# A pair of experts in which the transposes of the hidden rows move between two gathers and two down chunks change banks

## The chip, the cores and the metric

The kernel runs on one core of one Trainium2 chip. The metric is the device time of one execution in microseconds; of the kernel before, the median of three runs is 1393.09 us (1392.07 to 1394.43). TensorE (PE in the profile) multiplies matrices and writes to banks of PSUM; VectorE (DVE) and ScalarE (ACT) read the banks and write to SBUF; GpSimd (POOL) works on SBUF; SyncE (SP) issues the transfers from HBM.

## The reference, cut to what matters

The reference is one layer of a hybrid model on 256 tokens of width 2048: attention with compressed, selected and windowed keys beside a state-space mixer, an output projection with a norm, then a mixture of 32 experts and a second norm. The change lies in the experts. Each token is routed to two of the 32, and each expert is a gated unit of width 512:

```python
def expert_block(args):
    tok, e = args
    xb = h[tok]
    return (jax.nn.silu(xb @ w_gate[e]) * (xb @ w_up[e])) @ w_down[e]
...
out = jnp.zeros((n, d), jnp.float32).at[buf_tok].add(y.reshape(buf_len, d) * buf_w[:, None])
```

All of it is float32, and all 32 experts' weights are read: 3 x 2048 x 512 x 4 bytes each, 402.7 MB together.

## The kernel before, in words

The part ahead of the experts (projections, attention, state-space, output projection, first norm, routing) takes the first 425 us and is left as it is.

The experts are worked on in 16 pairs. Each expert has 64 slots for its tokens, so the two of a pair share the 128 columns or partitions of a tile. Tokens are picked by one-hot matrices: `one_hots(pr)` (line 1114 on) builds S, and `gather(xg, S, c)` (line 1120 on) multiplies the normed rows `hpm` by S into one bank, 16 records on TensorE for each quarter c of the model's width, and evicts the result with the norm's gain and offset into `xg`; VectorE evicts quarters 0 and 2, ScalarE quarters 1 and 3. A pair then runs, in the order in which the loop of line 1292 issues the work:

- the gate products `p_gate` and the up products `p_up` (line 1300), four chunks each of two weight tiles. An fp32 matmul shows as two records in the trace, so a chunk is 16 records and the eight chunks 128;
- `hidden` (line 1185 on), a generator in two steps. The first step is silu of the gate on ScalarE and the product with up on VectorE. The second transposes the result by four matmuls against the identity into the bank `p_ht` and copies it to `aT` on ScalarE;
- the first two quarters of the next pair's gather, between the generator's two steps;
- `weights_t` (line 1133 on): the one-hot matrices transposed and the slots' weights, by TensorE into the bank `p_sw`, and three copies on ScalarE to `swT` and `wsl`;
- four down chunks `p_dn` (line 1330), each with a matmul group into a bank, then `weighted` (lines 1152 and 1153: ScalarE scales by the slots' weights and rounds, VectorE keeps the rest) and, one chunk later, `combine` (lines 1161 and 1165: TensorE multiplies by `swT`, VectorE adds to the sums of the tokens). The next pair's quarters 2 and 3 are gathered behind the first and ahead of the last `combine`.

Each engine works through its instructions in the order of the program, so this order of issue is also each engine's queue. PSUM's eight banks are given out by tags, in turn within a tag: three "acc" (down chunks, combines), two "s" (gate, up), two "t" (gathers), one "o" (`p_ht`, `p_sw`). A matmul into a bank waits until its last reader is done.

The weights go through a ring of SBUF tiles of 1 MB (line 944 on). `ring_fill` issues on SP the next tiles as soon as a matmul chunk has used up others, so a transfer starts when a tile is free, up to a lane of semaphores: SP holds eight of these, and waits for the transfer that used the lane before. A pair has 24 tiles of 1024 KB. In the last pair the tiles are half as large, and the down chunks are eight of 256 columns. `besides` (line 1282) names work that is issued behind a chunk of the gate or up products, `weights_t` of the last pair among it.

Of the kernel before, what the change touches and what calls it, by code (L numbers as in the profile page):

```python
# [32 lines left out]
NE = 32  # L33
# [37 lines left out]
def block_kernel(ctx: ExitStack, tc: tile.TileContext, I: dict, out: bass.AP):  # L71
# [10 lines left out]
    def bank(tag, name, dt=F32):  # L82
        return ps.tile([P, 512], dt, name=name, tag=tag, bufs=BANKS[tag])
# [3 lines left out]
    def slot(i, name, dt=F32):  # L87
        if i > 20:
            return extra[0].tile([P, 2048], dt, name=name, tag=f"s{i}")
        return big.tile([P, 2048], dt, name=name, tag=f"s{i}")  # L90
# [263 lines left out]
    acc = {}  # L354
# [575 lines left out]
    LASTP = NE // 2 - 1  # L930
# [44 lines left out]
    def ring_take(*key):  # L975
        t, at = ring["tiles"].pop(key)
        shared = any(o == at for _, o in ring["tiles"].values())
        if at not in ACC and at != WORK and not shared:
            ring["free"].append(at)
        return t  # L980

    def ring_fill():
        while ring["next"] < len(items) and (ring["free"] or second(ring["next"])):
            ring_load()
# [71 lines left out]
    def residual(j, a):  # L1056

        c = j % 4
        v = acc[a][:, 512 * c:512 * c + 512]
        if j < 4:  # L1060
            t = v if c in FIRST else bank("acc", "p_rt")
            dve.tensor_tensor(t.rearrange("p (q k) -> p q k", k=KT), hv[a][:, 32 * c:32 * c + 32],
                              RES[j].rearrange("p (q k) -> p q k", k=KT), op=OP.mult)
            if c not in FIRST:
                dve.tensor_add(v, v, t)
        else:
            dve.tensor_tensor(v, v, RES[j], op=OP.add)
# [46 lines left out]
    def one_hots(pr):  # L1114
        S = mw.tile([P, 2, P], F32, name="S", bufs=2)
        dve.tensor_tensor(S.rearrange("p a (u s) -> p a u s", u=2), slots[:, None, None, :CAP].to_broadcast([P, 2, 2, CAP]),
                          R[:, :, 2 * pr:2 * pr + 2, None].to_broadcast([P, 2, 2, CAP]), op=OP.is_equal)
        SEL[pr] = S

    def gather(dst, S, c, tags=("t",)):  # L1120
        pgs = [bank(t, "p_g") for t in tags]
        at = lambda k: pgs[k * len(tags) // 4][:, k * P:(k + 1) * P]
        for k in range(4):
            for a in range(2):
                pe.matmul(at(k), hpm[a][:, 4 * c + k], S[:, a], start=(a == 0), stop=(a == 1))  # L1125
        for k in range(4):
            kk = 4 * c + k
            if c % 2:
                act.activation(dst[:, kk], at(k), AF.Identity, scale=ln1[:, 0, kk:kk + 1], bias=ln1[:, 1, kk:kk + 1])
            else:  # L1130
                dve.tensor_scalar(dst[:, kk], at(k), ln1[:, 0, kk:kk + 1], ln1[:, 1, kk:kk + 1], op0=OP.mult, op1=OP.add)

    def weights_t(pr):
        S = SEL.pop(pr)
        pt = bank("o", "p_sw")
        for a in range(2):
            pe.transpose(pt[:, a * P:(a + 1) * P], S[:, a], ident)
        for a in range(2):
            pe.matmul(pt[:, T:T + 2], S[:, a], wt[:, a, 2 * pr:2 * pr + 2], start=(a == 0), stop=(a == 1),
                      skip_group_check=True)  # L1140
        swT = mw.tile([P, T], F32R, name="swT")
        wsl = mw.tile([P, 1], F32, name="wsl")
        act.copy(swT, pt[:, :T])
        for u in range(2):
            act.copy(wsl[64 * u:64 * u + 64], pt[64 * u:64 * u + 64, T + u:T + u + 1])
        SW[pr] = swT, wsl

    def weighted(py, wsl, i):

        w = py.shape[-1]  # L1150
        hi, lo = [WK[0][:, 512 * j:512 * j + w] for j in (i % 2, 2 + i % 2)]
        act.activation(hi, py, AF.Copy, scale=wsl)  # L1152
        dve.scalar_tensor_tensor(lo, py, wsl, f(hi), op0=OP.mult, op1=OP.subtract)  # L1153
        return hi, lo

    def combine(swT, ys, lo, w, fin=None, init=False):
        s = slice(lo, lo + w)
        for a in range(2):
            pc = bank("acc", "p_co")[:, :w]
            for y, part in enumerate(ys):  # L1160
                pe.matmul(pc, swT[:, a * P:(a + 1) * P], part, start=(y == 0), stop=(y == 1))  # L1161
            if init:
                dve.tensor_copy(acc[a][:, s], pc)
            else:
                dve.tensor_add(acc[a][:, s], acc[a][:, s], pc)  # L1165
            if fin:
                for h in range(lo, lo + w, 256):
                    dve.bn_stats(st2[:, a, h // 256], acc[a][:, h:h + 256])
# [16 lines left out]
    def hidden(pg, pu, xg):  # L1185

        am, aT = xg[:, 8:12].rearrange("p k s -> p (k s)"), xg[:, 12:16]
        act.activation(am, pg, AF.Silu)  # L1188
        dve.tensor_mul(am, am, pu)  # L1189
        yield  # L1190
        pt = bank("o", "p_ht")
        for q in range(4):
            pe.transpose(pt[:, q * P:(q + 1) * P], am[:, q::4], ident)
        act.copy(aT, pt.rearrange("p (q s) -> p q s", q=4))
        yield aT
# [73 lines left out]
    def rows2(j):  # L1269
        if j % 4 == 0:  # L1270
# [10 lines left out]
    ring_fill()  # L1281
    besides = {(0, "g", 0): [(gather, xg, SEL[0], 1), (gather, xg, SEL[0], 2)], (0, "g", 1): [(gather, xg, SEL[0], 3)],
               (0, "u", 0): [(weights,)],
               (1, "u", 0): [(block_table,)], (LASTP, "u", 0): [(weights_t, LASTP)],
               (LASTP - 1, "g", 0): [(split_rows2,)]}
    for j in range(2, 8):
        besides[j, "g", 0] = [(res_rows, j)]
        besides[j, "g", 1] = [(residual, j, 0)]
# [3 lines left out]
    for pr in range(NE // 2):  # L1292
        pg, pu = bank("s", "p_gate"), bank("s", "p_up")
        for nm, pp in (("g", pg), ("u", pu)):
            for q in GU[pr == LASTP]:
                tl = [ring_take(nm, 2 * pr + u, q) for u in range(2)]
                for k in range(q[1]):
                    kk = q[0] + k
                    for u in range(2):
                        pe.matmul(pp[64 * u:64 * u + 64, :], xg[:, kk, 64 * u:64 * u + 64], tl[u][:, k],  # L1300
                                  start=(kk == 0), stop=(kk == KT - 1), skip_group_check=True)
                ring_fill()
                for fn, *args in besides.get((pr, nm, (q[0] + q[1]) / 4 - 1), []):
                    fn(*args)
        if pr < LASTP:
            one_hots(pr + 1)
        if pr == 0:
            WK[0] = slot(WORK, "work", F32R)
        xg = slot(XGS, "xg").rearrange("p (k s) -> p k s", s=P)
        hid = hidden(pg, pu, xg)  # L1310
        next(hid)
        if pr < LASTP:
            gather(xg, SEL[pr + 1], 0)
            gather(xg, SEL[pr + 1], 1)
        if pr == 0:
            for a in range(2):
                acc[a] = slot(ACC[a], f"sum{a}")
            for j in FIRST:
                for a in range(2):
                    residual(j, a)  # L1320
        aT = next(hid)
        if pr < LASTP:
            weights_t(pr)
        late = None
        for i, (c, lo, w) in enumerate(DOWN_LAST if pr == LASTP else DOWN):
            tl = [ring_take("d", 2 * pr + u, (lo, w)) for u in range(2)]
            py = bank("t" if pr == LASTP else "acc", "p_dn")[:, :w]
            for q in range(4):
                for u in range(2):
                    pe.matmul(py[64 * u:64 * u + 64, :], aT[:, q, 64 * u:64 * u + 64], tl[u][:, q], start=(q == 0),  # L1330
                              stop=(q == 3), skip_group_check=True)
            ring_fill()
            ys = weighted(py, SW[pr][1], i)
            if late:
                combine(*late)
            if pr < LASTP and c in (0, 3):
                gather(xg, SEL[pr + 1], 2 + (c == 3))
            late = (SW[pr][0], ys, lo, w, pr == LASTP, pr == 0 and c not in FIRST)
        if pr < LASTP:
            combine(*late)  # L1340
        else:
            combine_last(sums_first(*late[2:4]), *late[:4])
        SW.pop(pr)
# [5 lines left out]
    with tc.For_i(0, nblk, 1) as b:  # L1349
# [29 lines left out]
        for src, pp in ((wgate, pg), (wup, pu)):  # L1379
            for q in range(4):  # L1380
                t = slot(OVER[n % 4], "w_o")
                n += 1
                nc.sync.dma_start(t, src[bass.ds(e, 1), q].rearrange("o p x -> p (o x)"))
                t = t.rearrange("p (k f) -> p k f", f=FE)
# [3 lines left out]
        hid = hidden(pg, pu, slot(XGS, "oam").rearrange("p (k s) -> p k s", s=P))  # L1388
        next(hid)
        aT = next(hid)  # L1390
        for c in range(4):
            t = slot(OVER[n % 4], "w_o")
            n += 1
            nc.sync.dma_start(t, wdown[bass.ds(e, 1), c].rearrange("o p x -> p (o x)"))
            t = t.rearrange("p (f d) -> p f d", f=4)
            py = bank("acc", "p_dn")
# [96 lines left out]
```

## Time and profile before

| | |
|---|---|
| median of three runs | 1393.09 us |
| the profiled execution, its own time | 1393.33 us |
| its span | 1391.6 us |
| TensorE busy | 1312.2 us, 94% |
| VectorE, ScalarE, GpSimd busy | 513.8, 357.2, 154.1 us |
| gate, up and down products, busy | 225.9, 222.9, 241.4 us |
| gathers, busy | 127.2 us |
| read from HBM | 468.79 MB |
| weight tiles, of gate, up and down each | 120 of 1024 KB and 16 of 512 KB |

The span runs from the first to the last instruction; 1.73 us of the execution lie around it. A busy share is a mean over the whole program, whose stages have different limits: what a change in one of them is worth has to be read from that stage's own windows, waits and transfers. "Landing" is the time at which a transfer's semaphore tells that its bytes are there.

### The profile page before, as it was taken

The numbers are of one execution on the slowest core, as the hardware profiler recorded it, in microseconds if no ns is written. First come the engines' busy times: TensorE is split into PE (matmuls) and PEld (weight loads), VectorE is DVE, ScalarE is ACT, GpSimd is POOL, SyncE is SP. The second block draws the span as 40 slices with busy tenths as digits, with TensorE's granted clock in tenths as the row PEclk, the third lists the DMA queues.
The fourth block names the chain that finished last, engine by engine and source line by source line (L and its number), as shares of the span: only waits on it lengthen the run. The fifth ranks groups of instructions, "written<-read, shape, count | busy, mean of one in ns | idle before, by whom it ended". The sixth has DMA issues, their size and how long they took to land. (4 is left out here: it accounts for less than half of the span.)

```text
span 1391.6 us, 18135 instructions
## 1 busy us (share of the span) xinstructions
PE 1312.2 (94%) x7347; PEld 758.6 (55%) x7347; DVE 513.8 (37%) x1085; ACT 357.2 (26%) x687; POOL 154.1 (11%) x78
## 2 busy tenths in 40 slices
PE   7998999999999999999999999999999999999994
PEld 6778899997885434344344443444434444344432
DVE  6757676468833323131121312213122131221207
ACT  5554566455424102011010111101111011110112
POOL 2533233333520000000000000000000000000001
PEclk9999999999999999999999999999999999999997
DMA  8752334435798899999999999999999999999981
GB/s 314 288 177 91 122 103 141 152 122 212 302 412 342 350 391 421 421 421 421 421 421 421 421 421 421 421 421 421 421 421 421 421 421 421 421 420 421 407 325 61
DMA packets 70692, 472.10 MB, mean 339 GB/s; under 512 B 8510, under 2 KB 8766, under 8 KB 17102
## 3 DMA queue, kind: packets, MB, share of 16 engines
q1 hardware_dynamic: 70016, 470.75, 83.6%
q8 instruction: 59, 0.97, 0.3%
q10 hardware_dynamic: 590, 0.17, 0.1%
q14 instruction: 27, 0.22, 0.0%
HBM read 468.79 MB, written 2.10 MB: 338 GB/s over the span
## 5 line engine op out<-in xcount | busy, mean ns | idle before, releaser
L1330 PE MATMUL p_dn<-wd,xg 128*64 128x512 f32 (+1 forms) x1088 | 241.4, 587 | 14.9 <-DVE work L1153 14.3
L1300 PE MATMUL p_gate<-wg,xg 128*64 128x512 f32 x1024 | 225.9, 596 | 0.0
L1300 PE MATMUL p_up<-wu,xg 128*64 128x512 f32 x1024 | 222.9, 592 | 0.0
L222 POOL TENSOR_TENSOR w_lo<-raw,w_hi 128x1024 fp32r<-128x1024 f32 x52 | 141.4, 2721 | 258.4 <-ACT w_hi L221 245.8
L1189 DVE TENSOR_TENSOR xg<-xg,p_up 128x512 f32<-128x512 f32 x16 | 11.0, 688 | 394.1 <-ACT xg L1188 394.1
L1300 PEld LDWEIGHTS p_up<-wu,xg 128*64 128x64 f32 x1024 | 73.3, 137 | 145.5 <-issue 141.9
L1330 PEld LDWEIGHTS p_dn<-wd,xg 128*64 128x64 f32 x1088 | 73.7, 139 | 142.7 <-issue 108.0
L1300 PEld LDWEIGHTS p_gate<-wg,xg 128*64 128x64 f32 x1024 | 71.6, 137 | 143.7 <-issue 136.2
L1153 DVE SCALAR_TENSOR_TENSOR work<-p_dn,wsl,work 128x512 fp32r<-128x512 f32 (+1 forms) x68 | 48.9, 719 | 269.8 <-ACT work L1152 269.8
L1125 PEld LDWEIGHTS p_g<-S,hp 128*128 128x128 f32 x1024 | 120.8, 194 | 28.2 <-issue 26.0
L1125 PE MATMUL p_g<-S,hp 128*128 128x128 f32 x1024 | 127.2, 281 | 0.9 <-DVE cnt L1278 0.9
L221 ACT CAST w_hi<-raw 128x1024 fp32r<-128x1024 f32 (+1 forms) x112 | 109.0, 1027 | 36.9 <-issue 9.1
L1152 ACT ACTIVATE work<-p_dn,wsl 128x512 fp32r<-128x512 f32 (+1 forms) x68 | 45.2, 664 | 278.2 <-PE p_dn L1330 275.1
L1425 POOL TENSOR_TENSOR sum<-sum,row 128x512 f32<-128x512 f32 x4 | 6.7, 1691 | 972.3 <-DVE sum L1417 972.3
L310 PE MATMUL p_acc<-xh,w_hi 128*128 128x256 f32 x384 | 112.5, 293 | 0.0
L1188 ACT ACTIVATE xg<-p_gate 128x512 f32<-128x512 f32 x16 | 9.6, 597 | 391.7 <-PE p_up L1300 391.7
L312 PE MATMUL p_acc<-xl,w_hi 128*128 128x256 f32 x384 | 109.6, 285 | 0.0
L313 PE MATMUL p_acc<-xh,w_lo 128*128 128x256 f32 x384 | 109.6, 285 | 0.0
L222 DVE TENSOR_TENSOR w_lo<-raw,w_hi 128x1024 fp32r<-128x1024 f32 (+1 forms) x60 | 78.2, 1309 | 33.1 <-ACT w_hi L221 33.0
L1165 DVE TENSOR_TENSOR sum<-sum,p_co 128x512 f32<-128x512 f32 (+1 forms) x130 | 79.7, 650 | 9.5 <-PE p_co L1161 9.5
L1161 PE MATMUL p_co<-work,swT 128*128 128x512 f32 (+1 forms) x268 | 76.7, 408 | 0.0
L310 PEld LDWEIGHTS p_acc<-xh,w_hi 128*128 128x128 f32 x384 | 74.8, 195 | 0.7
(382 smaller groups left out, 1465.2 us busy)
## 6 DMA issues: line engine op xcount, KB each, us to landing
wg<-in_w_gate SPq DMA_DIRECT2D x120, 1024.0 KB, 15.3
wu<-in_w_up SPq DMA_DIRECT2D x120, 1024.0 KB, 17.7
wd<-in_w_down SPq DMA_DIRECT2D x120, 1024.0 KB, 11.7
raw<-in_w_dense SPq DMA_DIRECT2D x52, 1024.0 KB, 4.9
wg<-in_w_gate SPq DMA_DIRECT2D x16, 512.0 KB, 10.8
wu<-in_w_up SPq DMA_DIRECT2D x16, 512.0 KB, 10.2
wd<-in_w_down_last SPq DMA_DIRECT2D x16, 512.0 KB, 10.2
cw<-in_cmp_w SPq DMA_DIRECT2D x4, 1024.0 KB, 6.8
```

The source lines that it names most:

```text
L221: act.copy(hi[:, ks, :w], raw)
L222: eng.tensor_tensor(lo[:, ks, :w], raw, f(hi[:, ks, :w]), op=OP.subtract)
L310: pe.matmul(dst, hi[:, k, s], xk(xh, kt), start=(first and k == 0 and j % 2 == 0), stop=False, skip_group_check=True)
L312: pe.matmul(dst, hi[:, k, s], xk(xl, kt), start=False, stop=False, skip_group_check=True)
L313: pe.matmul(dst, lo[:, k, s], xk(xh, kt), start=False, stop=(last and k == 3), skip_group_check=True)
L1125: pe.matmul(at(k), hpm[a][:, 4 * c + k], S[:, a], start=(a == 0), stop=(a == 1))
L1152: act.activation(hi, py, AF.Copy, scale=wsl)
L1153: dve.scalar_tensor_tensor(lo, py, wsl, f(hi), op0=OP.mult, op1=OP.subtract)
L1161: pe.matmul(pc, swT[:, a * P:(a + 1) * P], part, start=(y == 0), stop=(y == 1))
L1165: dve.tensor_add(acc[a][:, s], acc[a][:, s], pc)
L1300: pe.matmul(pp[64 * u:64 * u + 64, :], xg[:, kk, 64 * u:64 * u + 64], tl[u][:, k], start=(kk == 0), stop=(kk == KT - 1), skip_group_check= ...
L1330: pe.matmul(py[64 * u:64 * u + 64, :], aT[:, q, 64 * u:64 * u + 64], tl[u][:, q], start=(q == 0), stop=(q == 3), skip_group_check=True)
```

## The change

It does three things in each pair. `aT = next(hid)`, with the transposes p_ht and their copy, moves from behind the two gathers to between them. `weights_t` moves from behind the gathers into the up products, behind their second chunk; in the last pair it moves there from behind the first. And the second and third down chunk (i of 1 and 2) take their banks from the tag "t", which the gathers use, in place of "acc".

```diff
     besides = {(0, "g", 0): [(gather, xg, SEL[0], 1), (gather, xg, SEL[0], 2)], (0, "g", 1): [(gather, xg, SEL[0], 3)],
                (0, "u", 0): [(weights,)],
-               (1, "u", 0): [(block_table,)], (LASTP, "u", 0): [(weights_t, LASTP)],
-               (LASTP - 1, "g", 0): [(split_rows2,)]}
+               (1, "u", 0): [(block_table,)], (LASTP - 1, "g", 0): [(split_rows2,)]}
+    for pr in range(NE // 2):
+        besides.setdefault((pr, "u", 1), []).append((weights_t, pr))
...
         if pr < LASTP:
             gather(xg, SEL[pr + 1], 0)
+        aT = next(hid)
+        if pr < LASTP:
             gather(xg, SEL[pr + 1], 1)
...
-        aT = next(hid)
-        if pr < LASTP:
-            weights_t(pr)
         late = None
         for i, (c, lo, w) in enumerate(DOWN_LAST if pr == LASTP else DOWN):
             tl = [ring_take("d", 2 * pr + u, (lo, w)) for u in range(2)]
-            py = bank("t" if pr == LASTP else "acc", "p_dn")[:, :w]
+            py = bank("t" if pr == LASTP or i in (1, 2) else "acc", "p_dn")[:, :w]
```

On TensorE, from a pair's up products to its first down chunk, the instructions stood in this order before (a matmul here is one instruction, which the trace shows as two records; a gather's matmuls alternate between two halves of the tokens and are cut here):

```order
L1300 MATMUL p_up<-wu,xg 64x512 x32
L1125 MATMUL p_g<-S,hp_4213 128x128
L1125 MATMUL p_g<-S,hp_4214 128x128
...
L1193 MATMUL p_ht<-ident,xg 128x128 x4
L1137 MATMUL p_sw<-ident,S 128x128 x2
L1139 MATMUL p_sw<-wt,S 128x2 x2
L1330 MATMUL p_dn<-wd,xg 64x512 x8
```

Here all sixteen of the two gathers' matmuls stand between the up products and p_ht, and p_sw follows p_ht. After the change:

```order
L1301 MATMUL p_up<-wu,xg 64x512 x16
L1137 MATMUL p_sw<-ident,S 128x128 x2
L1139 MATMUL p_sw<-wt,S 128x2 x2
L1301 MATMUL p_up<-wu,xg 64x512 x16
L1125 MATMUL p_g<-S,hp_4213 128x128
L1125 MATMUL p_g<-S,hp_4214 128x128
...
L1193 MATMUL p_ht<-ident,xg 128x128 x4
L1125 MATMUL p_g<-S,hp_4213 128x128
L1125 MATMUL p_g<-S,hp_4214 128x128
...
L1330 MATMUL p_dn<-wd,xg 64x512 x8
```

The four p_sw instructions now split the up products in halves, and p_ht has eight matmuls of a gather on either side.

On ScalarE the same stretch reads before (silu into xg, the eviction of the second gather, the copy of p_ht, the copies of p_sw, the scaling of the first down chunk):

```order
L1188 ACTIVATE xg<-p_gate 128x512 [waits PE_49,Activation_49]
L1129 ACTIVATE xg<-p_g,ln_127 128x128 [waits PE_49]
L1129 ACTIVATE xg<-p_g,ln_127 128x128 x3
L1194 COPY xg<-p_ht 128x512 [waits PE_49]
L1143 CAST swT<-p_sw 128x256 [waits PE_49]
L1145 COPY wsl<-p_sw 64x1 [waits DVE_49]
L1145 COPY wsl<-p_sw 64x1
L1152 ACTIVATE work<-p_dn,wsl 128x512 [waits PE_49,Activation_49]
```

and after:

```order
L1143 CAST swT<-p_sw 128x256 [waits PE_49]
L1145 COPY wsl<-p_sw 64x1 [waits DVE_49]
L1145 COPY wsl<-p_sw 64x1
L1188 ACTIVATE xg<-p_gate 128x512 [waits PE_49,Activation_49]
L1194 COPY xg<-p_ht 128x512 [waits PE_49]
L1129 ACTIVATE xg<-p_g,ln_127 128x128 [waits PE_49]
L1129 ACTIVATE xg<-p_g,ln_127 128x128 x3
L1152 ACTIVATE work<-p_dn,wsl 128x512 [waits PE_49,Activation_49]
```

The copies of p_sw now stand ahead of silu, and the copy of p_ht ahead of the second gather's eviction. The instructions of VectorE and of SP keep their order.

## Rows read from the trace of the kernel before

**Rows 1.** Windows: PE, PEld, DVE, ACT, POOL busy; granted clock, DMA share, GB/s.

```profile
540.00:1240.00 700.00, 669.90 (x3380) 295.68 (x3378) 148.99 (x277) 88.37 (x203) 0.00 (x0) 0.99 1.01 421
...
1290.00:1340.00 50.00, 48.55 (x226) 20.12 (x227) 9.22 (x16) 8.50 (x20) 0.00 (x0) 0.97 1.02 408
```

**Rows 2.** Timeline of TensorE: start, us, instructions; first gate products of pairs 8, 9.

```profile
910.47 13.95 PE L1300 MATMUL p_gate<-wg,xg 128*64 128x512 f32 x64
...
968.21 13.96 PE L1300 MATMUL p_gate<-wg,xg 128*64 128x512 f32 x64
```

**Rows 3.** Up tiles of pair 14: issues on SP, first and last, landing.

```profile
L971 SPq DMA_DIRECT2D wu<-in_w_up x8: 327/328/328, 1234.3 to 1251.7; - x8
...
DMA to landing us min/median/max: 19.8/19.8/19.8
```

**Rows 4.** The same for the up tiles of pair 15, the last.

```profile
L971 SPq DMA_DIRECT2D wu<-in_w_up x16: 327/328/328, 1303.0 to 1322.1; - x16
...
DMA to landing us min/median/max: 10.2/10.2/10.2
```

**Rows 5.** Timeline of TensorE, end of pair 14's up products, and pair 15.

```profile
1284.58 3.84 PE L1125 MATMUL p_g<-S,hp 128*128 128x128 f32 x32
...
1340.59 7.09 PE L1300 MATMUL p_up<-wu,xg 128*64 128x512 f32 x32
1349.15 0.75 PE L1193 MATMUL p_ht<-ident,xg 128*128 128x128 f32 x4 [1.48 <-DVE xg L1189]
1350.58 3.67 PE L1330 MATMUL p_dn<-wd,xg 128*64 128x256 f32 x32 [0.68 <-ACT xg L1194]
...
1367.58 1.95 PE L1330 MATMUL p_dn<-wd,xg 128*64 128x256 f32 x16
```

**Rows 6.** Timeline of TensorE, pair 4: gathers to the third down chunk.

```profile
700.09 3.84 PE L1125 MATMUL p_g<-S,hp 128*128 128x128 f32 x32
703.76 0.64 PE L1193 MATMUL p_ht<-ident,xg 128*128 128x128 f32 x4
706.00 0.44 PE L1137 MATMUL p_sw<-ident,S 128*128 128x128 f32 x2 [1.60 <-ACT xg L1194]
...
706.71 5.35 PE L1330 MATMUL p_dn<-wd,xg 128*64 128x512 f32 x16
...
719.23 3.65 PE L1330 MATMUL p_dn<-wd,xg 128*64 128x512 f32 x16 [0.48 <-DVE work L1153]
```

**Rows 7.** Waits of TensorE from 560 to the end: total us, times, longest.

```profile
PE p_sw L1137 <- ACT xg L1194: 20.8, 13, 1.6
PE p_dn L1330 <- DVE work L1153: 12.4, 26, 0.5
```

**Rows 8.** Timeline of ScalarE, pair 1, between up and down products.

```profile
525.41 1.51 ACT L1129 ACTIVATE xg<-p_g,ln 128x128 f32<-128x128 f32 x4 [3.08 <-PE p_g L1125]
526.80 0.60 ACT L1194 COPY xg<-p_ht 128x512 f32<-128x512 f32 x1
```

**Rows 9.** Timeline of VectorE and ScalarE in pair 0.

```profile
448.12 0.25 DVE L1221 SCALAR_TENSOR_TENSOR wt<-wt,wb,Mb 128x32 f32<-128x32 f32 x1
...
463.95 1.28 ACT L1188 ACT_TABLE_LOAD   x1 [17.68 <-PE p_up L1300]
```

**Rows 10.** A window of pair 4's first down chunk, columns as in rows 1.

```profile
708.00:710.00 2.00, 2.00 (x6) 0.49 (x4) 0.00 (x0) 0.00 (x0) 0.00 (x0) 0.50 1.00 418
```

**Rows 11.** Windows around the last idle time of the transfers.

```profile
494.00:500.00 6.00, 6.00 (x30) 2.00 (x32) 5.48 (x22) 0.61 (x2) 0.00 (x0) 1.00 0.66 250
500.00:506.00 6.00, 6.00 (x32) 2.00 (x30) 0.24 (x1) 0.00 (x0) 0.00 (x0) 1.00 1.03 429
```

**Rows 12.** The down tiles of pair 15: issues on SP, landing.

```profile
L968 SPq DMA_DIRECT2D wd<-in_w_down_last x16: 327/328/328, 1323.4 to 1342.6; - x16
...
DMA to landing us min/median/max: 10.1/10.2/10.2
```

**Rows 13.** Landing of the up tiles issued between 895 and 936.

```profile
DMA to landing us min/median/max: 11.9/12.9/13.9
```

## The prediction

> **What bounds the kernel now.** I read the page's slices first, to see which resource is full where; the expert stage has two, and the windows put numbers on them. From 540 to 1240 the transfers run at 421 GB/s, a DMA share of 1.01, and TensorE is busy for 669.90 of 700 us; in the last pair, whose tiles are half as large, it is 408 GB/s [rows 1]. So the question is on which of the two the end hangs. The chain of waits does not tell: it is followed back only through the norm behind the experts. A pair of experts moves 24 tiles of 1.0486 MB, 25.17 MB, so the transfers need 25.17 MB / 421 GB/s = 59.8 us for a pair. TensorE needs less: pair 8 begins its gate products at 910.47 and pair 9 at 968.21, 57.7 us later [rows 2]. TensorE is late in the pipeline only because it started with a full ring of weights waiting; it catches up with the transfers by some 2 us in each of these pairs.
>
> How far is it still behind? A tile has landed at its issue plus the time to landing. In pair 14 the last tile of the up products is issued at 1251.7; tiles of 1 MB take 19.8 us to land there, so it lies ready at 1271.5 [rows 3]. TensorE ends those products at 1284.58 and the chunk that uses the tile (16 of 64 records, 3.5 us) starts at 1281.1 [rows 5]: **a lead of 9.6 us**. In pair 15 the last up tile is issued at 1322.1 and ready 10.2 later, at 1332.3 [rows 4]; the last quarter of the 32 records that start at 1340.59 starts at 1345.8 [rows 5]: **a lead of 13.5 us**. So the end is TensorE's today, but with the transfers close behind, and they are a wall.
>
> **The change part by part.** *The removed wait.* In a pair TensorE runs both gathers (3.67 us for 32 records), the four transposes p_ht, and then sits idle for 1.60 us before p_sw [rows 6]; the engine's waits list 13 of these, 20.8 us, put down to the copy of p_ht [rows 7]. ScalarE's rows tell why: the copy of p_ht (526.80) stands behind the eviction of the second gather, 1.51 us from 525.41 [rows 8]. From the up products' end to the first down product it takes 706.71 - 700.09 = 6.62 us. After the change p_sw is inside the up products, where it costs its own 0.71 us (706.71 - 706.00), and then come half a gather 1.84, p_ht 0.6, half a gather 1.84: 0.71 + 4.3 = 5.0. **Saved: 1.6 us.** What must hide for that: in the last pair, which has no gather, p_ht starts 1.47 us after the up products end (1347.68 to 1349.15: silu, the product with up) and the down products 1.43 after p_ht starts [rows 5]. The first gather covers the one by 0.4 us, p_ht and the second gather (2.4) cover the other by 1.0. If the first cover failed by as much as it now holds, 0.4 us a pair would come back.
>
> *The two banks.* The third down chunk waits 0.48 us for VectorE to read the bank that it reuses [rows 6], and the fourth as long: 26 waits, 12.4 us [rows 7], 0.95 a pair. With chunks 1 and 2 in the gathers' banks, chunk 1 needs the second gather evicted (1.51 us [rows 8], while the first down chunk and a gather run for over 5), chunk 2 needs gather 2 evicted (a down chunk and a combine, 4.8 us, lie between), and the fourth chunk comes back to a bank that a combine left one chunk before. That leaves no new wait that I can see; the bounds are the two waits of 0.48 us gone, or both there again elsewhere. **Saved: 0.95 us.** The moved p_sw is copied by ScalarE in the up products, when it has nothing queued, and needs the pair's weights from VectorE: even in pair 0 these are written by 448.4, before the up products begin [rows 9]. SP's queue is unchanged and has none of the moved work.
>
> So a pair costs TensorE 2.55 us less, about 55.2. In pair 0 the silu brings a table load of 1.28 us [rows 9] that the first gather alone does not cover: 0.9 is lost, and 0.7 + 0.95 = 1.65 is saved. Over pairs 0 to 14 that is 1.65 + 14 x 2.55 = **37 us of TensorE's time**. [...]
>
> **But the wall stands.** The transfers can't end much earlier: they last stood idle between 494 and 500 (250 GB/s in that window, 429 and more behind it [rows 11]), when the ring was full and SP waited for pair 1's first gate chunk. That moment comes earlier by what pair 0 saves, 1.65 us (bounds 0.95, if nothing but the bank waits goes, and 2.55), and with it all later landings. From there they are saturated, so TensorE can move forward only by the lead plus 1.65:
> - to the last up chunk of pair 14: 9.6 + 1.65 = 11.2. Its own savings up to there are over 33, so it will have been waiting for weights since about pair 9, where the lead (some 2 us more for each pair back) meets what has been saved.
> - from there to the last up chunk of pair 15, TensorE saves p_sw behind the gathers, 6.62 - 4.3 = 2.3, the bank waits 0.95, and 1.7 if pair 14's half-clock chunk is gone too: 14.5 to 16.2 in all.
> - the wall there: 13.5 + 1.65 = 15.15.
> Behind it all goes on as before: the last down tile is issued at 1342.6 and ready at 1352.8 [rows 12], its chunk starts at 1367.6 [rows 5], a lead of 14.8 that moves along with the same 1.65.
>
> So the end moves by 14.5 to 15.15 us; I take 14.8. No row shows how long TensorE takes to start after a landing that it waited for; between nothing and the 0.68 us that it stood for the copy of p_ht at 1350.58 [rows 5] I take 0.4 off: **14.4 us**. Against the profiled execution, 1391.6 of span and 1393.33 in all, that is 1377.2 and 1378.9. The median of 1393.09 is 0.24 lower, so the forecast is **1378.7 us**, 1.0% faster, though TensorE gets rid of 37 us or more.
>
> **The rivals.**
> *Transfers could go faster (1349 to 1356 us, chance 0.04).* If 421 GB/s were what TensorE asks for, an earlier free slot would bring faster transfers, and the full 37 to 44 us would be had. Against it: the rate is 421 in one stretch in which up tiles take 12.9 us to land (895 to 936) and 19.8 (from 1234 on), so a longer queue brought nothing [rows 1, 3, 13].
> [...]
>
> *Something takes the saving back (1381 to 1385, chance 0.10).* If p_ht or its copy waits anyway and only the 0.95 for the banks is real, 15 pairs still give 14, the wall at pair 14 leaves 9.6 + 0.95 = 10.6, and 0.95 follows: 11.5, or 1381.6. With half of that a pair, 1386. It takes a failure of nearly the whole edit to come below 5 us, because only 15 of 37 are needed.
>
> *Waiting for weights costs the clock.* Today idle times of 1.60 us brought the clock down in some pairs. Starved, TensorE waits 59.8 - 55.2 = 4.6 us a pair, about 1.5 in each of the last three up chunks. The pairs before the last absorb that in their slack; a fall from pair 14's last up chunk on does not go away and costs 1.7 us. One or two of them: 1380 to 1382 (chance 0.12). **The slower side** is the same mechanism in force: over the seven starved pairs it must eat 4.6 us of slack each and the 14.4 won, 6.7 us a pair, four falls in each, where today one pair in three has one. Five falls a pair (8.5 us) would give 1391.6 - 14.4 + 7 x 3.9 + 1.7 = 1406. Chance 0.04.
> [...]
>
> *Nothing happens (1390 to 1395, chance 0.04).* If the transfers already set the end, no TensorE time would count. The 13.5 us between the last up tile's landing and its use speak against it.
>
> **How the numbers follow.** Forecast 0.66, faster transfers 0.04, partial loss 0.10, one or two clock falls 0.12, no change 0.04, slower 0.04. The range takes the forecast with the bounds of the transfers' shift (0.95 to 2.55) and the mild clock case: 1376.5 to 1382.5. About 0.2% is what a measurement of this kernel can tell from no change; faster by more has 0.66 + 0.04 + 0.10 + 0.12 = 0.92.
>
> **What would show it.** Right: no idle time between p_ht and the down products, none before the third and fourth chunk; a period of 59.8 us from about pair 10 on; up products that wait for in_w_up; transfers at 421 GB/s and ending about 1.6 us earlier; last matmul near 1357. Wrong: a period under 59 us in pairs 10 to 14 (the wall is soft); idle time before p_ht or p_dn as before (the cover failed); granted clock far below 0.98 from 1000 on (the clock rival).

## The result, and the profile after

The changed kernel takes 1378.35 us, the median of four runs (1377.56 to 1379.17), where the kernel before takes 1393.76 beside it; the ratio is 0.9889 with a 95% interval of 0.9872 to 0.9906. The forecast was 1378.7 in 1376.5 to 1382.5. The profiled execution has a span of 1376.0 us; the tables below are of it.

Between a pair's up products and its first down chunk TensorE no longer stands still. The timeline of TensorE in pair 1 (start, us, instructions; compare [rows 6]):

```profile
504.72 7.04 PE L1301 MATMUL p_up<-wu,xg 128*64 128x512 f32 x32
...
512.40 7.09 PE L1301 MATMUL p_up<-wu,xg 128*64 128x512 f32 x32
519.42 2.05 PE L1125 MATMUL p_g<-S,hp 128*128 128x128 f32 x16
521.31 0.64 PE L1193 MATMUL p_ht<-ident,xg 128*128 128x128 f32 x4
521.79 1.95 PE L1125 MATMUL p_g<-S,hp 128*128 128x128 f32 x16
523.67 3.65 PE L1330 MATMUL p_dn<-wd,xg 128*64 128x512 f32 x16
527.25 2.05 PE L1125 MATMUL p_g<-S,hp 128*128 128x128 f32 x16
529.23 3.65 PE L1330 MATMUL p_dn<-wd,xg 128*64 128x512 f32 x16
532.82 1.20 PE L1161 MATMUL p_co<-work,swT 128*128 128x512 f32 x4
533.94 3.65 PE L1330 MATMUL p_dn<-wd,xg 128*64 128x512 f32 x16
```

From the gathers' start to the first down chunk it is 4.25 us (6.62 before), and from the second down chunk to the third 4.71 (5.26 before). No row has a releaser: nothing waits. The up products, which now hold p_sw, take 519.42 - 504.72 = 14.70 us, 0.87 more than the 521.54 - 507.71 = 13.83 of before:

```profile
507.71 13.90 PE L1300 MATMUL p_up<-wu,xg 128*64 128x512 f32 x64
521.54 3.84 PE L1125 MATMUL p_g<-S,hp 128*128 128x128 f32 x32
```

On ScalarE the copy of p_ht now stands ahead of the eviction (compare [rows 8]):

```profile
521.99 0.59 ACT L1194 COPY xg<-p_ht 128x512 f32<-128x512 f32 x1 [1.77 <-PE p_ht L1193]
523.77 1.51 ACT L1129 ACTIVATE xg<-p_g,ln 128x128 f32<-128x128 f32 x4 [1.20 <-PE p_g L1125]
```

What took the place of the waits, in the waits of TensorE from 560 to the end (total us, times, longest; compare [rows 7]):

```profile
PE p_up L1301 <- DMA wu<-in_w_up: 15.7, 14, 1.3
PE p_ht L1193 <- DVE xg L1189: 1.5, 1, 1.5
PE p_dn L1330 <- ACT xg L1194: 0.7, 1, 0.7
```

The two waits inside a pair are gone; the last two rows are the last pair's, as before. New are fourteen waits for up tiles. They begin in pair 9, and from there the pairs run at the pace of the transfers. The timeline of TensorE, pairs 9, 11 and 14 and the start of 15:

```profile
959.34 3.65 PE L1301 MATMUL p_up<-wu,xg 128*64 128x512 f32 x14 [1.20 <-DMA wu<-in_w_up]
969.28 3.65 PE L1301 MATMUL p_up<-wu,xg 128*64 128x512 f32 x14 [1.15 <-DMA wu<-in_w_up]
...
1078.99 3.65 PE L1301 MATMUL p_up<-wu,xg 128*64 128x512 f32 x14 [1.32 <-DMA wu<-in_w_up]
1088.93 3.65 PE L1301 MATMUL p_up<-wu,xg 128*64 128x512 f32 x14 [1.15 <-DMA wu<-in_w_up]
...
1239.62 13.95 PE L1301 MATMUL p_gate<-wg,xg 128*64 128x512 f32 x64
...
1299.50 13.95 PE L1301 MATMUL p_gate<-wg,xg 128*64 128x512 f32 x64
```

Pair 14 lasts 1299.50 - 1239.62 = 59.88 us: the transfers' 59.8, and no longer TensorE's own. A wait here falls inside a chunk: two records use the first expert's tile, and the other fourteen wait for the second's. The last pair's up tiles (issues on SP, landing; compare [rows 4]) and TensorE's rows around them (compare [rows 5]):

```profile
L971 SPq DMA_DIRECT2D wu<-in_w_up x16: 327/328/328, 1300.8 to 1319.9; - x16
DMA to landing us min/median/max: 10.1/10.2/10.2
```

```profile
1323.69 6.24 PE L1301 MATMUL p_up<-wu,xg 128*64 128x512 f32 x26
1330.14 1.93 PE L1301 MATMUL p_up<-wu,xg 128*64 128x512 f32 x6 [0.21 <-DMA wu<-in_w_up]
1333.54 0.75 PE L1193 MATMUL p_ht<-ident,xg 128*128 128x128 f32 x4 [1.47 <-DVE xg L1189]
1334.97 3.67 PE L1330 MATMUL p_dn<-wd,xg 128*64 128x256 f32 x32 [0.68 <-ACT xg L1194]
...
1351.97 1.95 PE L1330 MATMUL p_dn<-wd,xg 128*64 128x256 f32 x16
```

The last up tile lands at 1319.9 + 10.2 = 1330.1, and TensorE goes on at 1330.14: the lead is used up to the last tenth. From p_ht to the end it is 42.5 us in both executions (1391.6 - 1349.15 and 1376.0 - 1333.54).

The transfers run at the rate of before (columns as in [rows 1]):

```profile
540.00:1240.00 700.00, 687.02 (x3434) 306.85 (x3432) 154.41 (x286) 92.12 (x209) 0.00 (x0) 1.00 1.01 421
```

The granted clock is 1.00 where 0.99 stood, though TensorE waits again.

### The profile page after: what moved, and what is told of

Read it like the earlier page. It is cut to its first block, busy times and chain, and to the rows that moved or that the text cites. A ratio compares the mean times of both kernels' runs of the same rounds, so it can differ in the third digit from the quotient of the medians.

```text
span 1376.0 us, 18148 instructions
## 1 busy us (share of the span) xinstructions
PE 1318.3 (96%) x7347; PEld 763.6 (55%) x7347; DVE 514.1 (37%) x1085; ACT 358.7 (26%) x687; POOL 154.0 (11%) x78
## 5 line engine op out<-in xcount | busy, mean ns | idle before, releaser
L1301 PE MATMUL p_up<-wu,xg 128*64 128x512 f32 x1024 | 241.3, 596 | 15.7 <-DMA wu<-in_w_up 15.7
L1330 PE MATMUL p_dn<-wd,xg 128*64 128x512 f32 (+1 forms) x1088 | 234.6, 573 | 0.7 <-ACT xg L1194 0.7
L1301 PEld LDWEIGHTS p_up<-wu,xg 128*64 128x64 f32 x1024 | 80.8, 137 | 158.7 <-issue 114.7
L1143 ACT CAST swT<-p_sw 128x256 fp32r<-128x256 f32 x16 | 6.0, 372 | 328.4 <-PE p_sw L1139 328.4
L222 DVE TENSOR_TENSOR w_lo<-raw,w_hi 128x1024 fp32r<-128x1024 f32 (+1 forms) x60 | 78.3, 1310 | 32.7 <-ACT w_hi L221 32.5
## 6 DMA issues: line engine op xcount, KB each, us to landing
wu<-in_w_up SPq DMA_DIRECT2D x16, 512.0 KB, 10.2
```

The costliest lines, as they stand in the source:

```text
L222: eng.tensor_tensor(lo[:, ks, :w], raw, f(hi[:, ks, :w]), op=OP.subtract)
```

## The experiments

Two theories. **W**, the prediction's: the transfers are a wall some 14 us behind the end of before, and TensorE's time counts only up to it. **P**: the end is the sum of TensorE's time, in the changed kernel too; the change is worth 15 us because TensorE really saves no more. Of the changed kernel there are 13 runs in all, those of the two repeats below among them, with a mean of 1378.62 us (standard error 0.42).

### Each half of the change alone

The banks alone, on the kernel before:

```diff
-            py = bank("t" if pr == LASTP else "acc", "p_dn")[:, :w]
+            py = bank("t" if pr == LASTP or i in (1, 2) else "acc", "p_dn")[:, :w]
```

> The kernel before with the bank change alone (down chunks 1 and 2 in the gathers' banks), transposes and one-hot transposes where they were. Theory W (the transfers are a wall that lies 13.5 us behind the end of before): TensorE saves about 1.05 us a pair, 16 us over pairs 0 to 14; the wall lets through 9.6 + 1.1 at pair 14's last up chunk and 1.1 more after it, so 11.8 us faster than before (10 to 13.5). Theory P (the end is the sum of TensorE's time, and the whole change is worth 15 us because TensorE really saves no more): the banks' share is 1.05 of 2.65, so 6 us.

Measured: 1383.12 us, ratio 0.9921 (0.9894 to 0.9949), 10.6 us faster. The moves alone are the changed kernel with that line put back:

> The changed kernel with the down chunks' banks as before: only the transposes between the gathers and the one-hot transposes in the up products. W: TensorE saves 1.6 us a pair, 24 us, and the wall lets through 9.6 + 0.6 at pair 14 and 2.3 to 4.0 behind it, at most 14.1: 12.5 to 14.1 us faster than before. P: the share of 1.6 of 2.65, 9 us. By W this run and the banks alone add up to about 25 us, by P to 15.

Measured: 1378.44 us, ratio 0.9885 (0.9869 to 0.9902), 15.3 us faster, more than the 12.5 to 14.1 that W had said for it. **The halves add up to 26 us, the whole is worth 15.** The moves alone already reach the wall; the waits of TensorE in that kernel from 560 on:

```profile
PE p_dn L1330 <- DVE work L1153: 12.3, 26, 0.5
PE p_up L1301 <- DMA wu<-in_w_up: 6.1, 6, 1.3
```

The bank waits are still there and TensorE waits for weights besides: removing the first only lengthens the second (6.1 us here, 15.7 in the changed kernel). With the banks alone, however, TensorE does not wait for weights at all: the last up tile lands at 1330.2 and is used some 3 us later. So W's number came out by luck; the wall is not what held this kernel back. TensorE saves 15 x 1.10 = 16.5 us there, but in the profiled execution nine chunks run at half clock, by their length (5.27 to 5.36 us, where 3.65 to 3.67 is usual; granted clock 0.97 from 900 to 1300), where before had four: eight of the fifteen that follow the 1.60 us wait, and the first down products of the last pair. Five more at 1.7 us each leave 16.5 - 8.5 = 8.0. The other 3.0 of the 11.0 by which its span of 1380.6 is shorter have nothing to do with the change: pair 0 begins at 427.17 instead of 429.23, and its first gate chunk takes 3.65 us instead of 4.54. The first gate chunk, four of the nine and a normal one (938.58) in its timeline:

```profile
427.17 3.65 PE L1300 MATMUL p_gate<-wg,xg 128*64 128x512 f32 x16
...
467.46 5.35 PE L1330 MATMUL p_dn<-wd,xg 128*64 128x512 f32 x16
...
931.31 5.35 PE L1330 MATMUL p_dn<-wd,xg 128*64 128x512 f32 x16
938.58 3.65 PE L1330 MATMUL p_dn<-wd,xg 128*64 128x512 f32 x16
...
989.66 5.35 PE L1330 MATMUL p_dn<-wd,xg 128*64 128x512 f32 x16
...
1337.93 5.36 PE L1330 MATMUL p_dn<-wd,xg 128*64 128x256 f32 x32 [0.68 <-ACT xg L1194]
```

### More work for TensorE

The same matmuls as a quarter of a gather, into a bank that nobody reads, 1.98 us in each of pairs 1 to 13, 25.7 us in all:

```diff
+    def extra_work(pr):
+        p = bank("t", "p_x")
+        for k in range(4):
+            for a in range(2):
+                pe.matmul(p[:, k * P:(k + 1) * P], hpm[a][:, k], SEL[pr][:, a], start=(a == 0), stop=(a == 1))
+    for pr in range(1, LASTP - 1):
+        besides.setdefault((pr, "g", 0), []).append((extra_work, pr))
```

> The changed kernel with 16 more gather records (about 1.95 us of TensorE, into a bank that nobody reads) behind the first gate chunk of pairs 1 to 13, 25 us in all. W: hidden in the waits for weights; within 1.5 us of the changed kernel (1378 to 1380). P: 25 us slower than the changed kernel, 1403.

> The same 25 us of added TensorE work in the kernel before. Both theories: TensorE sets the end there and has no waits for weights, so 23 to 26 us slower than before, 1416 to 1419. If it were hidden here too, the work would cost less than its records say and the run on the changed kernel would prove nothing.

Measured: on the changed kernel 1381.06 us, ratio 0.9902 (0.9886 to 0.9919), 2.4 us over the changed kernel's mean; on the kernel before 1423.93, ratio 1.0216 (1.0199 to 1.0233), **30.2 us slower**. The same work costs all of its time and more in one kernel and a tenth of it in the other. In the changed kernel the 2.4 us are more than the 1.5 that W allowed; in the profiled execution the last up tile landed 904.1 us behind pair 0's first gate product, and 902.6 on average in three profiles of the changed kernel, so the transfers too were 1.5 us later. The work fills the waits: they fall from fourteen to two, and a window in the starved stretch shows TensorE without a gap, where the changed kernel (last line) has one (columns as in [rows 1]):

```profile
PE p_up L1309 <- DMA wu<-in_w_up: 2.3, 2, 1.2
```

```profile
900.00:1100.00 200.00, 200.00 (x1035) 89.66 (x1035) 36.47 (x69) 24.30 (x58) 0.00 (x0) 1.00 1.01 421
```

```profile
900.00:1100.00 200.00, 192.71 (x960) 87.48 (x956) 36.92 (x71) 25.82 (x60) 0.00 (x0) 1.00 1.01 421
```

On the kernel before I had expected 23 to 26 us. What comes on top is the clock, as far as a trace shows it: in the profiled execution (granted clock 0.979, where before has 0.985) eight down chunks take 5.35 us, not four, and 25.7 + 4 x 1.7 = 32.5 of the 33.3 us by which that execution (1427.03 us) is longer. The other three runs lie 3 us lower, at a granted clock of 0.982 to 0.983 instead of 0.979; fewer such chunks would explain it, but they have no trace. Three of the eight:

```profile
959.10 5.35 PE L1338 MATMUL p_dn<-wd,xg 128*64 128x512 f32 x16
...
1020.70 5.35 PE L1338 MATMUL p_dn<-wd,xg 128*64 128x512 f32 x16
...
1082.28 5.35 PE L1338 MATMUL p_dn<-wd,xg 128*64 128x512 f32 x16
```

### Fewer transfers

One tile in 24 is left out in pairs 1 to 14, and the first expert's tile is used twice in its place (so the output is another); TensorE's work stays:

```diff
+        if 0 < pr < LASTP:
+            dn.pop()
...
-            tl = [ring_take("d", 2 * pr + u, (lo, w)) for u in range(2)]
+            if i == 3 and 0 < pr < LASTP:
+                tl = [ring_take("d", 2 * pr, (lo, w))] * 2
+            else:
+                tl = [ring_take("d", 2 * pr + u, (lo, w)) for u in range(2)]
```

> The changed kernel with one weight tile less in pairs 1 to 14: the fourth down chunk of the second expert is not loaded, and both experts use the first one's tile (the output of those columns is another). TensorE's work is the same. W: the wall recedes by 14 tiles of 2.49 us, 35 us, TensorE no longer waits and all that it saves shows: 44 to 46 us faster than before (37 of removed waits and 7 of half clock, a little more for the banks), 1347 to 1353. P: as the changed kernel, 1378. If 421 GB/s was no limit: 1378 too.

> The same tile left out in the kernel before. W and P: TensorE sets the end, so within 2 us of before. If fewer transfers as such made TensorE faster (less contention for SBUF), 5 us or more faster, and part of the gain of the run on the changed kernel would be that.

Measured: the changed kernel 1348.76 us, ratio 0.9683 (0.9668 to 0.9698), **44.2 us faster than before**; the kernel before 1392.58, ratio 1.0001 (0.9992 to 1.0011), nothing. These are the runs that settle it. Without the wall all of TensorE's saving shows: 14 pairs at 57.74 - 55.14 = 2.60 us, 1.56 in pair 0 and four half-clock chunks of 1.7 are 44.8 us, and from pair 0's first gate product to the last pair's p_ht it is 875.09 us instead of 919.92, 44.83 less. In the kernel before, where TensorE sets the end, they are worth nothing, and fewer transfers did not make TensorE itself faster either: it is busy for 669.90 us from 540 to 1240, as with all tiles [rows 1]. In the changed kernel with fewer tiles TensorE is never idle from 540 to 1240, and a pair takes 940.64 - 885.50 = 55.14 us; the windows of it, and of the kernel before with the same tiles left out:

```profile
540.00:1240.00 700.00, 700.00 (x3550) 307.86 (x3551) 157.87 (x292) 93.58 (x213) 0.00 (x0) 1.00 1.01 421
```

```profile
540.00:1240.00 700.00, 669.90 (x3370) 295.46 (x3368) 148.60 (x275) 88.34 (x203) 0.00 (x0) 0.99 1.00 409
```

The second also says what 421 GB/s is: where TensorE frees tiles more slowly than that, the rate falls to what it frees, 409 here and 411 in the kernel before with the added work. In the twelve other profiles it is 421 from 540 on (422 in one window of 60 us), in the kernels that wait for weights and in those that do not yet. What SP waits for tells the two cases apart: from 540 to 1240, in the kernel before with fewer tiles nearly always for TensorE to free a tile, in the changed kernel (last two lines) mostly for earlier transfers. The costliest wait of each kind in either:

```profile
SPq L973 <- PE p_dn L1335: 164.5, 23, 10.9
SPq L973 <- DMA wg<-in_w_gate: 6.9, 11, 1.4
```

```profile
SPq L971 <- DMA wg<-in_w_gate: 188.2, 90, 3.3
SPq L968 <- PE p_gate L1301: 23.4, 12, 6.6
```

P and "421 is no limit" both expected 1378 for the changed kernel with fewer tiles and are out.

### Moving the wall

If the transfers set the end, their last idle time (around 470 to 500, when the ring is full) should be worth its length. Three quarters of pair 1's gather go behind pair 1's gate chunks, so that pair 0 frees its tiles earlier:

```diff
-        if pr < LASTP:
+        if pr == 0:
+            besides[1, "g", 0] = [(gather, xg, SEL[1], 1), (gather, xg, SEL[1], 2)]
+            besides[1, "g", 1] = [(gather, xg, SEL[1], 3)]
+        elif pr < LASTP:
             gather(xg, SEL[pr + 1], 1)
...
-            if pr < LASTP and c in (0, 3):
+            if 0 < pr < LASTP and c in (0, 3):
```

> The changed kernel again, beside the runs below on the same chip: 1378.4, 14 to 16 us faster than before.

> The changed kernel with quarters 1 to 3 of pair 1's gather moved from pair 0 behind pair 1's first and second gate chunks (as pair 0's own already are): the same instructions, but pair 0's down chunks and pair 1's first gate chunk come 2 to 5.7 us earlier and free their tiles earlier, when the transfers last stand idle. The p_ht copy is covered by less there (up to 1 us of TensorE idle in pair 0). W: what the transfers stand idle less around 470 to 500 comes off the end, 2 to 4 us, so 1374.5 to 1376.5. P: no TensorE work is saved, 0 to 1 us slower than the changed kernel.

> The changed kernel a third time, for an interval against the two runs below: 1378 to 1380.

> The kernel with pair 1's gathers late, again. W: 2 to 3 us faster than the changed kernel, about 1376.5. P: no difference.

Measured: the changed kernel again 1379.6 and 1378.21 us; with the gathers late 1376.88 and 1378.8. Nine runs have a mean of 1378.21 (standard error 0.58), the changed kernel's thirteen 1378.62. A further kernel has the late gathers and, besides, loads the table of silu while ScalarE is idle:

```diff
+    def silu_table():
+        warm = small_t("warm", [1])
+        act.activation(warm, epsc, AF.Silu)
...
-               (0, "u", 0): [(weights,)],
+               (0, "u", 0): [(weights,), (silu_table,)],
```

> Pair 1's gathers late and, besides, a one-column silu behind the weights of pair 0, so that the table is loaded while ScalarE is idle and the 0.78 us that TensorE waits for pair 0's product goes. W: another 0.8 us off, 3 to 4 us faster than the changed kernel, about 1375.5. P: 0.8 us.

> The kernel with pair 1's gathers late and the table of silu loaded early, again. W: its profiles so far put the end 3 us earlier, counted from pair 0's first gate product; the median of its runs should come to about 1376. P: as the changed kernel, 1378.6.

Measured: 1377.49 and 1376.24 us; eight runs with a mean of 1377.12 (standard error 0.66), 1.5 us under the changed kernel, with an interval of about -0.2 to 3.2. **This stays open**: the profiles go the way of W, the times don't resolve it. Transfers in the changed kernel and in this one (first profile), from 464 to 512:

```profile
464.00:512.00 48.00, 47.22 (x244) 21.20 (x242) 19.94 (x45) 7.61 (x15) 0.00 (x0) 1.00 0.92 368
```

```profile
464.00:512.00 48.00, 46.85 (x239) 20.71 (x239) 19.89 (x45) 6.43 (x14) 0.00 (x0) 1.00 0.97 390
```

22 GB/s more over 48 us is 1.06 MB, one tile, 2.5 us; but the repeats differ too, 377 GB/s for this kernel and 362 and 367 for the changed one. From pair 0's first gate product to the last pair's p_ht it is 905.6, 907.5 and 905.3 us in the three profiles of the changed kernel, 904.0 and 905.2 with the gathers late and 902.7 and 903.5 with the table too. I had expected 2 to 4 us from the gathers; the profiles show about 1.5, and the transfers, once let go earlier, run at only 295 GB/s between 494 and 500, where the changed kernel has 351.

## Why the prediction was right

Step by step, as it was put.

- **A pair costs TensorE 2.55 us less, about 55.2.** Right: 55.14 us where nothing waits, 2.60 less. The removed wait saved 6.62 - 4.25 - 0.87 = 1.50 rather than 1.6, since p_sw costs 0.87 us inside the up products and not its own 0.71; the banks saved 1.10 a pair rather than 0.95, since a chunk that need not wait also starts closer behind the combine ahead of it (5.26 to 4.71, twice).
- **Pair 0 saves 1.65.** Its length, first gate product to pair 1's, fell from 64.69 to 62.96: 1.73. Of this 0.17 is the first gate chunk (4.54 to 4.37 us), which the change does not touch; 1.56 is left.
- **Pair 14's half-clock chunk, 1.7 us, is gone too.** In the kernel before, the down chunks from 587.11, 706.71, 826.31 and 1291.21, each behind p_sw and its wait of 1.60 us, take 5.33 to 5.35 us where 3.65 is usual: 1.7 us each, 6.8 in all, the 7 between 37 and 44 us. The clock granted inside them ([rows 10] for the second; columns as in [rows 1]):

```profile
588.00:590.00 2.00, 2.00 (x8) 0.67 (x6) 0.00 (x0) 0.00 (x0) 0.00 (x0) 0.52 1.00 418
...
828.00:830.00 2.00, 2.00 (x8) 0.50 (x6) 0.00 (x0) 0.00 (x0) 0.00 (x0) 0.50 1.01 422
...
1292.00:1294.00 2.00, 2.00 (x8) 0.65 (x6) 0.00 (x0) 0.00 (x0) 0.00 (x0) 0.50 1.02 410
```

Right in the three profiles of the changed kernel; the four are gone and none came. The last pair keeps its waits of 1.47 and 0.68 us, though, and in two other kernels (the banks alone and the repeat of the late gathers) the down products behind them were slow in the same way: 5.36 us for 32 records in the first, 4.60 for the 26 that start before 1340 in the second, where 32 take 3.67. Why the changed kernel was spared no run shows.
- **TensorE waits for weights from about pair 9.** Right: the first wait with a releaser is at 959, in pair 9.
- **The wall at the last up tile, 13.5 us behind.** Right in place, and the start behind it costs 0.45 us where 0.4 was taken off (the last six records take 1.93 us from their start to the products' end, where the same six took 1.48). The lead itself was 0.43 us more than reckoned: the last tile is the second expert's, is used two records later, and it is this one that TensorE waits for. From pair 0's first gate product to the last p_ht the time fell by 919.92 - 905.56 = 14.36 us, against 14.4 forecast. So close a hit is luck: the lead was put 0.43 too low, the next term 0.7 too high, and 14.8 had been taken where the wall's own sum was 15.15.
- **The transfers' own end moves 1.65 us.** This is the term that was mis-sized, as far as three profiles against one of before can tell. In the profiled execution it moved 2.2 (1332.3 to 1330.1), but 1.25 of that is the part ahead of the experts, which ran quicker that time (pair 0's first gate product at 427.98, not 429.23) and has nothing to do with the change. Counted from that product it moved 0.95, and in the two repeats -0.9 and 1.3: a mean of 0.45. So a pair 0 that is 1.56 us shorter did not bring the end of the transfers forward by as much. Why is not shown; the moved p_sw, which delays the release of the later up tiles by its 0.87 us, and a second idle time of the transfers are candidates that no run separates. That the median lies 0.35 us below the forecast and not 1 us above it is within the scatter of the runs.

The rivals: transfers that go faster are out (421 GB/s in every kernel that waits for weights). The clock did not fall in the starved pairs: it is granted at 1.00 from 954 to 1335.
The fourteen waits that the trace lists, up to 1.3 us with longer work between them (8.8 us from 959.34 to the wait ahead of 969.28), brought no fall; of the fifteen waits of 1.60 us in the kernel before, four did.

## What to carry to other kernels

Where two resources are nearly full, work out for the slower one's last use how long its operand has been lying there: that lead, and not the sum of removed waits, bounds what a change can bring (here 14 of 44 us). To prove which of the two sets the end, take work from one of them in both kernels: a tile in 24 less was worth nothing before the change and 30 us after it. Halves of a change that add up to more than the whole point to a wall, but each half needs its own trace: the moves alone had reached it, and the banks alone had not.

## What the runs showed of the hardware that I had not expected

- The DMA share does not tell that the transfers are at their limit. It is 1.00 at 409 and 411 GB/s, with SP waiting for free tiles, and 1.01 at 421. The rate tells, and whether SP waits for earlier transfers or for TensorE.
- The same idle time costs the clock in some pairs and not in others, and how often goes with the whole program. Each of the kernels without the moves has fifteen waits of 1.59 or 1.60 us; half-clock chunks (5.33 to 5.35 us instead of 3.65, with a granted clock of 0.50 to 0.52 inside them) follow four of them in the kernel before, and chunks of that length five with fewer tiles, eight with the banks alone and eight with the added work. Within a stretch they come whole pairs apart: 58.35 us with the banks alone (931.31 to 989.66) and 61.6 with the added work (959.10, 1020.70, 1082.28) are one pair, 119.6 in the kernel before (587.11, 706.71, 826.31) two, and 184.5 with the added work ahead of that (591.15, 775.65, 959.10) three. But stretches also end: with the banks alone six pairs in a row are spared between 525.81 and 931.31. What decides it no run shows. It is why one profile of such a kernel says little about its other runs.
- A wait for weights shows only in part as idle time. The six starved pairs from 939.88 to 1299.50 take 59.94 us on average instead of 55.14, 28.8 us in all; the list has 15.7. The rest lies in longer chunks: the 18 records at 1073 took 4.49 us, where 16 take 3.65 and two more 0.43, and the 14 behind a wait take 3.65, as much as 16 in the flow.
